# Both tiles' statistics in one group, and one GpSimd product moved to VectorE, in a two-layer diffusion trunk

## The chip, the cores and the metric

One core of one Trainium2 chip runs the whole program in one launch. The metric is device microseconds of one execution. A profiled execution records each engine: TensorE (PE, with its weight loads as PEld), VectorE (DVE), ScalarE (ACT), GpSimd (POOL) and SyncE (SP), which issues DMAs.

## The reference, cut to what matters

Two layers run over 128 prompt tokens and 1024 sample tokens, in float32, with model width 1024. Layer 0 mixes tokens by softmax attention (8 heads) beside a bidirectional gated linear attention (4 heads); layer 1 mixes by a convolution module. A SwiGLU FFN follows each. Every sub-layer begins with a modulation:

```python
def rmsnorm(x, g):
    y = xf * lax.rsqrt(jnp.mean(xf * xf, axis=-1, keepdims=True) + EPS)
    return (y * g.astype(jnp.float32)).astype(x.dtype)
def modulate(x, g, shift, scale):
    return rmsnorm(x, g) * (1 + scale) + shift
```

In the linear attention, per chunk, queries and keys are multiplied by exponentials of summed log gates: `scores = einsum('bhid,bhjd,bhijd->bhij', qc, kc, decay)` with `decay = exp(cum_i - cum_j)`.

## The kernel before, in words

Tokens lie along the free dimension: 1152 tokens are four tiles of 288 columns (after the convolution 280, 280, 296, 296), tiles 0 and 1 being group GA and tiles 2 and 3 group GB. The 1024 features are eight k-blocks of 128 partitions. Every float32 product is three matmuls over operands split in a high and a low part (`mm3`, L161 to L163); a weight block arrives by DMA on SyncE (`wraw`), ScalarE casts it to `wH` (L156), VectorE or GpSimd subtracts to get `wL` (L157).

`modulate` handles a group's two tiles one after the other. Per tile, `x_stats` squares the eight k-blocks on ScalarE (L369, L372) and adds them on VectorE (L373) into a tile `ssum` (two buffers); `bcast_rstd` sums over partitions with small matmuls against ones (L188), takes the reciprocal square root of a few columns (L191, L174 to L179), and spreads it over the partitions with small matmuls against the identity (L196) into a bank of `m` (two PSUM banks in these stages). Then `affine` makes `hH` and `hL` for the eight k-blocks (L381 to L391). The squares and the affine share a scratch tile `tmp` with four buffers. There are six such modulations after layer 0's mix, two tiles each: layer 0 FFN for GA and GB, layer 1 mix for GA and GB, layer 1 FFN for GA and GB.

In `layers`, layer 0's FFN for GA runs in six chunks of hidden blocks; GB's modulation stands after the second. Beside it VectorE sums the modulation parameters from streamed weights (`ada`, L292). Layer 1's convolution has a first product `pw1` with eight blocks f, each followed by a convolution that VectorE does tap by tap (L1275) and that is handed out in portions (`drip`); the FFN of the other group covers it.

In the attention stage (about 490 to 890 us of the span) the main loop is the softmax attention of a head; the linear attention `gla_b` is braided in, one chunk t of 128 tokens after the other (nine chunks). For each of two feature blocks f, ScalarE fills `kq` with exponentials (L904, L911), then `kq` is multiplied in place by the queries and keys: slots 0 to 6 by one product (L913, 896 elements per partition: on VectorE for f = 0, on GpSimd for f = 1), slots 7 to 15 by another (L915, 1152 elements, VectorE). TensorE takes both in the score matmuls (L928), whose results VectorE gathers in `pt` (L931, L933).

A framework sets the order of each engine's instructions at compile time: from the order in the program and from its own estimate of when each operand is ready. An instruction can be moved ahead of earlier ones where the estimate says that it is ready. On the chip each engine then works through its queue in that order, and an instruction that waits holds up those behind it.

Of the kernel before, what the change touches and what calls it, by code (L numbers as in the profile page):

```python
# [14 lines left out]
AF = mybir.ActivationFunctionType  # L15
ALU = mybir.AluOpType
AX = mybir.AxisListType

P = 128
D = 1024  # L20
KD = D // P
# [5 lines left out]
GA, GB = (0, 1), (2, 3)  # L27
# [20 lines left out]
R_PW, R_FF0, R_FF1 = 4, (5, 3), (4, 2)  # L48
# [9 lines left out]
EPS = 1e-6  # L58
# [58 lines left out]
class Trunk:  # L117
# [273 lines left out]
            nc.vector.scalar_tensor_tensor(L[:, k, s:e], t[:, s:e], sh[:, k, g:g + 1], H[:, k, s:e].bitcast(F32),  # L391
                                           op0=ALU.add, op1=ALU.subtract)

    def modulate(self, X, l, which, tts):
        nc = self.nc
        sh, a = self.par[l][3 * which], self.par[l][3 * which + 1]
        hs = {}
        for tt in tts:
            w = X[tt].shape[2]
            bc = self.x_stats(X, tt)  # L400
            H, L = self.h_tiles(tt, w)
            for k in range(KD):
                self.affine(tt, k, X[tt][:, k, :], bc, H, L, sh, a, MODS[k])
            hs[tt] = (H, L)
        return hs
# [467 lines left out]
    def gla_b(self, t):  # L873
        nc, kg, S, tb = self.nc, self.kg, self.S, self.gb
        fs, bs = kg[:, 0:1024], kg[:, 1024:2048]
        NL = len(LEVELS)
        tok = slice(t * P, (t + 1) * P)
        gqk = self.t(tb, [P, 4, P], "gqk", 2)
# [12 lines left out]
        for f in range(2):  # L891
            kq = self.t(tb, [P, 2 * NL + 2, P], "kq", 3)
            for d in range(2):
                src = fs if d == 0 else bs
                for half in range(2):
                    E = self.bank("g")
                    for i, L in enumerate((laH, laL)):
                        nc.tensor.matmul(E, L[:, d * 256 + f * P:d * 256 + (f + 1) * P],
                                         src[:, half * 512:half * 512 + 512], start=(i == 0), stop=(i == 1))
                    for q in range(4):  # L900
                        l = half * 4 + q
                        iv = E[:, q * P:(q + 1) * P]
                        if l == NL:
                            nc.scalar.activation(kq[:, 2 * NL + d, :], iv, AF.Exp)  # L904
                            continue
                        s = LEVELS[l]
                        base = kq[:, l, :] if d == 0 else kq[:, l, s:]
                        st = NL * P + s if d == 0 else NL * P - s
                        ov = bass.AP(base.tensor, base.offset,
                                     [list(base.ap[0]), [st, 2], [2 * s, 64 // s], [1, s]])  # L910
                        nc.scalar.activation(ov, iv.rearrange("p (a b c) -> p a b c", a=2, c=s), AF.Exp)  # L911
                    yield
            (nc.gpsimd if f else nc.vector).tensor_mul(kq[:, 0:NL], kq[:, 0:NL], gqk[:, f, :].unsqueeze(1).to_broadcast([P, NL, P]))  # L913
            yield
            nc.vector.tensor_mul(kq[:, NL:], kq[:, NL:],  # L915
                                 gqk[:, 2 + f, :].unsqueeze(1).to_broadcast([P, NL + 2, P]))
            KQ.append(kq)
            yield
# [19 lines left out]
        for f in range(2):  # L938
            for hp in range(2):
                h = f * 2 + hp  # L940
                nc.tensor.matmul(Ob[hp][:, f, :], PT[hp][:, f, :], gv[:, h * GDV:(h + 1) * GDV],
                                 start=True, stop=(t == 0))
            for d in range(2 if t > 0 else 0):
                for hp, r in enumerate(half):
                    nc.tensor.matmul(Ob[hp][:, f, :], KQ[f][r, 2 * NL + d, :], S(d, t)[r, f, :],
                                     start=False, stop=(d == 1))
        yield
        ss = self.t(tb, [P, GH], "gss", 2)
# [360 lines left out]
    def pw1(self, hs, grp, rate):  # L1309
        nc = self.nc  # L1310
        w1 = self.A["conv_w_pw1"][0].rearrange("(k p) f -> p k f", p=P)
        first = grp is GA
        x, C = self.x_group(T2, grp)
        for f in range(KD):
            bH, bL = self.wtile(w1[:, :, D + f * P:D + (f + 1) * P])
            aH, aL = self.wtile(w1[:, :, f * P:(f + 1) * P])
            u = self.t(self.up, [P, max(UA, UB)], f"u{f}")
            if first:
                nc.gpsimd.memset(u[:, 0:CPAD], 0.0)
                nc.gpsimd.memset(u[:, CPAD + P:2 * CPAD + P], 0.0)  # L1320
            else:
                nc.scalar.copy(u[:, 0:HALO], self.halo[:, f, :])
                nc.gpsimd.memset(u[:, UB - CPAD:UB], 0.0)
            for tt in grp:
                hH, hL = hs[tt]
                w = hH.shape[2]
                ba, bb = self.bank("a")[:, :w], self.bank("a")[:, :w]
                for k in range(KD):
                    self.mm3(bb, bH[:, k], bL[:, k], hH[:, k], hL[:, k], k == 0, k == KD - 1)
                for k in range(KD):  # L1330
                    self.mm3(ba, aH[:, k], aL[:, k], hH[:, k], hL[:, k], k == 0, k == KD - 1)
                sg = self.ev()[:, :w]
                nc.scalar.activation(sg, bb, AF.Sigmoid, bias=self.b_pw1[:, KD + f:KD + f + 1])
                a0 = T1[tt][0]
                parts = [(CPAD, 0, P), (2 * CPAD + P, P, w)] if tt == 0 else \
                    [(a0 + 2 * CPAD if first else a0 - (N2 - CPAD), 0, w)]
                for d, s, e in parts:
                    nc.vector.scalar_tensor_tensor(u[:, d:d + e - s], ba[:, s:e], self.b_pw1[:, f:f + 1],
                                                   sg[:, s:e], op0=ALU.add, op1=ALU.mult)
                self.drip(rate)  # L1340
            if first:
                nc.scalar.copy(self.halo[:, f, :], u[:, UA - HALO:UA])
                self.conv_taps(u, f, [(x[:, f, 0:P], 0), (x[:, f, P:], CPAD + P)])
            else:
                self.conv_taps(u, f, [(x[:, f, :], 0)])
        return C

    def x_load(self, X, grp):
        x, xs = self.x_group(T2, grp)
# [3 lines left out]
    def layers(self, X, hs):  # L1353
        nc, A = self.nc, self.A
        pa = self.pool("act")
        self.wpool = WPOOL[1]
        NB = max(C0A + C0B + C1A + C1B)
        cut = lambda ns: list(zip(np.cumsum((0,) + ns).tolist(), ns))
        chunks = cut(C0A)
        self.adq = nc.sync  # L1360
        self.ada_pin = ADA_PIN
        self.adp = self.pool("ada1", "right")
        self.ada_bufs = AB[2]
        gate = self.ada_seq(0, (5,), 512)
        self.pend.extend([lambda: next(gate, None)] * 20)
        ada = self.ada_seq(1, (1, 0, 2, 4, 3, 5), 512)
        for f0, n in chunks:
            for _ in range(-(-120 // len(chunks))):
                self.pend.append(lambda: next(ada, None))
            self.ffn(X, hs, 0, GA, f0, n, pa, NB, ADA_RATE if f0 else (4, 4))  # L1370
            self.drip(10 ** 6)
            if f0 == chunks[1][0]:
                hs.update(self.modulate(X, 0, 1, GB))
        self.adp.release()
        self.wpool = 0
        gate = self.par[1][2]
        nc.vector.tensor_mul(self.bg, gate, self.b_pw2.unsqueeze(2).to_broadcast([P, KD, 2]))
        w2 = A["conv_w_pw2"][0].rearrange("(k p) f -> p k f", p=P)
        self.up = self.pool("u", "right")
        self.halo = self.t(self.up, [P, KD, HALO], "halo")  # L1380

        hs.update(self.modulate(X, 1, 0, GA))
        self.x_dma(self.xg[0], 0, True)
        chunks = cut(C0B)
        self.ffn(X, hs, 0, GB, *chunks[0], pa, NB)
        C = self.pw1(hs, GA, R_PW)
        for c in chunks[1:-1]:
            self.ffn(X, hs, 0, GB, *c, pa, NB, R_FF0)
        self.drip(10 ** 6)
        self.wpool = WPOOL[3]  # L1390
        us = self.layer_norm(C, GA)
        self.ffn(X, hs, 0, GB, *chunks[-1], pa, NB)
        X2 = {}
        self.x_load(X2, GA)

        hs.update(self.modulate(X, 1, 0, GB))
        self.x_dma(self.xg[1], N1, True)
        self.proj_add(X2, us, w2, GA, gate, self.bg)
        h2 = self.modulate(X2, 1, 1, GA)
        C = self.pw1(hs, GB, R_PW)  # L1400
        chunks = cut(C1A)
        for c in chunks[:-2]:
            self.ffn(X2, h2, 1, GA, *c, pa, NB, R_FF1)
        self.drip(10 ** 6)
        self.wpool = WPOOL[3]
        us = self.layer_norm(C, GB)
        self.x_load(X2, GB)
        self.ffn(X2, h2, 1, GA, *chunks[-2], pa, NB)
        self.proj_add(X2, us, w2, GB, gate, self.bg)
        h2.update(self.modulate(X2, 1, 1, GB))  # L1410
        self.ffn(X2, h2, 1, GA, *chunks[-1], pa, NB)
        self.store_y(X2, GA)
        self.wpool = WPOOL[4]
        self.up.release()
        for c in cut(C1B):
            self.ffn(X2, h2, 1, GB, *c, pa, NB)
        self.store_y(X2, GB)
        pa.release()
# [55 lines left out]
```

## Time and profile before

| | |
|---|---|
| median of three runs | 3096.03 us (3094.78 to 3100.07) |
| the profiled execution | 3098.96 us |
| its span, first to last instruction | 3097.2 us |
| TensorE matmuls busy | 3002.1 us, 97% |
| VectorE busy | 2169.4 us, 70% |
| ScalarE busy | 1232.1 us, 40% |
| GpSimd busy | 405.2 us, 13% |
| mean granted TensorE clock | 0.984 |

Times in rows count from the span's start, in microseconds. A busy share is a mean over stages; what a change is worth is read at the waits of the engine that sets the end. An arrow `<-` behind a wait names what ended it.

### The profile page before, as it was taken

What the parts mean: (1) busy time and instruction counts of PE and PEld (TensorE: products, weight loads), DVE (VectorE), ACT (ScalarE), POOL (GpSimd) and SP (SyncE); (2) the same over time, 40 slices, a digit from 0 to 9 for tenths busy, and PEclk for the clock granted to TensorE, in tenths of its full rate; (3) what the DMA queues carried; (4) which work ended last, traced back from release to release, by engine and by line L of the source; (5) the groups of instructions that cost most, each with busy time, mean ns of one, the idle gap of its engine ahead of it and who ended that gap; (6) DMA issues with size and microseconds to landing.
All of it is one profiled execution on the core that took longest, in us unless ns stands there. A gap on an engine that the chain in (4) does not pass through costs nothing.

```text
span 3097.2 us, 53660 instructions
## 1 busy us (share of the span) xinstructions
PE 3002.1 (97%) x21044; PEld 2813.7 (91%) x21044; DVE 2169.4 (70%) x4110; ACT 1232.1 (40%) x2652; POOL 405.2 (13%) x371
## 2 busy tenths in 40 slices
PE   7999999999989999999999999999999999999999
PEld 4999866666769999999999999999999999999998
DVE  6668478788769999634679996667888875433343
ACT  5323377566664333223422223562222255222222
POOL 1012121112120111111111110111111010000000
PEclk9999999999999999999999999999999999999999
DMA  7545522111164555423232222522322231322222
GB/s 266 169 120 149 156 88 70 55 46 52 26 188 151 168 157 155 127 82 103 80 86 83 78 82 76 149 69 83 89 86 86 83 113 51 110 82 83 81 86 78
DMA packets 449631, 320.46 MB, mean 103 GB/s; under 512 B 29646, under 2 KB 413907, under 8 KB 449378
## 3 DMA queue, kind: packets, MB, share of 16 engines
q1 hardware_dynamic: 411726, 271.06, 29.3%
q0 software_dynamic: 8944, 30.68, 3.1%
q10 hardware_dynamic: 28708, 15.29, 1.7%
q8 instruction: 166, 2.72, 0.4%
q14 instruction: 87, 0.71, 0.1%
HBM read 278.30 MB, written 38.67 MB: 102 GB/s over the span
## 4 chain that ended last, share of the span: by engine, by line
PE 75%; DVE 13%; ACT 5%; DMA 3%; issue 3%; POOL 0%; SPq 0%; ACTq 0%; DVEq 0%; POOLq 0%
PE ps_a L161 16%; PE ps_a L163 16%; PE ps_a L162 16%; PE ps_d L162 3%; PE ps_d L163 3%; PE ps_d L161 3%; DVE y L1275 2%; PE ps_g L928 2%; PE ps_a L538 2%; PE ps_a L540 2%; PE ps_a L539 2%; DVE ada L292 1%; DVE wL L157 1%; DVE x L409 1%; PE ps_c L1236 1%
## 5 line engine op out<-in xcount | busy, mean ns | idle before, releaser
L163 PE MATMUL ps_a<-hH,wL 128*128 128x288 f32 (+2 forms) x3328 | 985.3, 296 | 6.7 <-DVE wL L157 6.7
L161 PE MATMUL ps_a<-hH,wH 128*128 128x288 f32 (+2 forms) x3328 | 983.9, 296 | 1.8 <-ACT wH L156 1.8
L162 PE MATMUL ps_a<-hL,wH 128*128 128x288 f32 (+2 forms) x3328 | 985.2, 296 | 0.0
L156 ACT CAST wH<-wraw 128x1024 fp32r<-128x1024 f32 (+3 forms) x432 | 362.4, 843 | 768.4 <-PE ps_a L162 480.7
L163 PEld LDWEIGHTS ps_a<-hH,wL 128*128 128x128 f32 x3328 | 627.7, 189 | 8.0 <-DVE wL L157 7.8
L161 PEld LDWEIGHTS ps_a<-hH,wH 128*128 128x128 f32 x3328 | 629.0, 189 | 2.6 <-ACT wH L156 2.3
L162 PEld LDWEIGHTS ps_a<-hL,wH 128*128 128x128 f32 x3328 | 627.5, 189 | 0.2
L157 DVE TENSOR_TENSOR wL<-wraw,wH 128x1024 fp32r<-128x1024 f32 (+3 forms) x349 | 336.0, 965 | 130.2 <-ACT wH L156 129.3
L1275 DVE SCALAR_TENSOR_TENSOR y<-u,cvw,y 128x575 f32<-128x575 f32 (+1 forms) x464 | 420.1, 905 | 8.4
L157 POOL TENSOR_TENSOR wL<-wraw,wH 128x1024 fp32r<-128x1024 f32 (+2 forms) x83 | 172.7, 2081 | 975.3 <-ACT wH L156 975.1
L161 PE MATMUL ps_a<-aH,wH 128*128 128x288 f32 (+2 forms) x880 | 259.8, 296 | 0.2 <-ACT wH L156 0.2
L163 PE MATMUL ps_a<-aH,wL 128*128 128x288 f32 (+2 forms) x880 | 259.0, 295 | 0.0
L162 PE MATMUL ps_a<-aL,wH 128*128 128x288 f32 (+2 forms) x880 | 258.9, 294 | 0.0
L448 DVE TENSOR_TENSOR ev<-ev,ps_a 128x288 f32<-128x288 f32 (+2 forms) x176 | 79.3, 450 | 226.9 <-PE ps_a L163 225.6
L292 DVE SCALAR_TENSOR_TENSOR ada<-ada,scc,ada 128x512 f32<-128x512 f32 (+1 forms) x364 | 219.7, 647 | 20.0 <-DMA ada<-in_w_ada 19.8
L156 ACT CAST aH<-ev 128x288 fp32r<-128x288 f32 (+2 forms) x176 | 75.9, 431 | 330.7 <-DVE ev L448 329.1
L161 PEld LDWEIGHTS ps_a<-aH,wH 128*128 128x128 f32 x880 | 165.9, 189 | 0.5 <-ACT wH L156 0.5
L162 PEld LDWEIGHTS ps_a<-aL,wH 128*128 128x128 f32 x880 | 166.1, 189 | 0.0
L163 PEld LDWEIGHTS ps_a<-aH,wL 128*128 128x128 f32 x880 | 165.5, 188 | 0.5 <-DVE wL L157 0.5
L161 PE MATMUL ps_d<-aH,wH 128*128 128x288 f32 (+2 forms) x528 | 158.3, 300 | 6.3 <-ACT wH L156 3.5
L161 PE MATMUL ps_d<-hH,wH 128*128 128x288 f32 (+2 forms) x512 | 153.2, 299 | 8.6 <-DVE dr L1248 6.6
L409 DVE SCALAR_TENSOR_TENSOR x<-ps_a,par,x 128x288 f32<-128x288 f32 (+5 forms) x300 | 128.5, 450 | 45.8 <-PE ps_a L163 45.1
(338 smaller groups left out, 5770.7 us busy)
## 6 DMA issues: line engine op xcount, KB each, us to landing
wraw<-in_ffn_w_gate SPq DMA_DIRECT2D x88, 512.0 KB
wraw<-in_ffn_w_up SPq DMA_DIRECT2D x88, 512.0 KB
wraw<-in_ffn_w_down SPq DMA_DIRECT2D x144, 256.0 KB
ada<-in_w_ada SPq DMA_DIRECT2D x112, 256.0 KB
wraw<-in_conv_w_pw SPq DMA_DIRECT2D x48, 512.0 KB
in<-in_w_ada SPq DMA_DIRECT2D x8, 1024.0 KB
ada<-in_w_ada SPq DMA_DIRECT2D x64, 128.0 KB
wraw<-in_w_out SPq DMA_DIRECT2D x16, 512.0 KB
```

What stands on the lines that cost most here:

```text
L156: self.nc.scalar.copy(H, src)
L157: (eng or self.nc.vector).tensor_sub(L, src, H.bitcast(F32))
L161: mm(out, WH, hH, start=start, stop=False)
L162: mm(out, WH, hL, start=False, stop=False)
L163: mm(out, WL, hH, start=False, stop=stop)
L292: ins = self.nc.vector.scalar_tensor_tensor(acc[v], w, s, acc[v], op0=ALU.mult, op1=ALU.add)
L409: self.nc.vector.scalar_tensor_tensor(X[tt][:, o, s:e], src[:, s:e], gate[:, o, g:g + 1], X[tt][:, o, s:e], op0=ALU.mult, op1=ALU.add)
L448: nc.vector.tensor_mul(pr, sl, bu)
L538: mm(b[:, :wd], hh, wh, start=(k == 0), stop=False)
L539: mm(b[:, :wd], hh, wl, start=False, stop=False)
L540: mm(b[:, :wd], hl, wh, start=False, stop=(k == KD - 1))
L1275: pin(nc.vector.scalar_tensor_tensor(d, u[:, i + o:i + o + w], c, y[:, o:o + w], op0=ALU.mult, op1=ALU.add))
```

## The change

Two independent edits. `modulate` now takes the squares and sums of both tiles first (`sums`), then treats them in one group (`pair_bcast`): one set of small matmuls, one square root and one chain of short VectorE instructions over the columns of both tiles, and two broadcast banks. In two of the six places the halves are pulled apart: for GB in layer 0 the sums stand after the second FFN chunk and the rest after the third; for GA in layer 1's FFN the sums stand before the second `pw1` and the rest after its first block, for which `pw1` has become a generator. In `gla_b`, the product of L913 is on VectorE for both f.

```diff
+    def pair_bcast(self, sums, w):
...
+        st = self.bank()
+        for i, s in enumerate(sums):
+            for j in range(n):
+                o = 2 * (i * n + j)
+                nc.tensor.matmul(st[:c, o:o + 2], s[:, j * c:(j + 1) * c], self.ones[:, 0:2], start=True, stop=True)
+        m = n * len(sums)
+        tmp = self.tmp()
+        v, r, q = (tmp[:c, i:i + m] for i in (0, 8, 16))
...
+        nc.scalar.activation(q, v, AF.Sqrt)
+        nc.vector.reciprocal(r, q)
...
+        for i in range(len(sums)):
+            bc = self.bank()
+            for j in range(n):
+                nc.tensor.matmul(bc[:, j * c:(j + 1) * c], r[:c, i * n + j:i * n + j + 1].to_broadcast([c, P]),
+                                 self.ident[:c, :c], start=True, stop=True)
...
+    def sums(self, X, tts):
...
+            nc.scalar.activation(ssum, x[:, 0, :], AF.Square)
+            for k in range(1, KD):
+                sq = self.tmp()[:, :w]
+                nc.scalar.activation(sq, x[:, k, :], AF.Square)
+                nc.vector.tensor_add(ssum, ssum, sq)
...
-    def modulate(self, X, l, which, tts):
+    def modulate(self, X, l, which, tts, ss=None):
...
-        for tt in tts:
+        ss = ss or self.sums(X, tts)
+        for tt, bc in zip(tts, self.pair_bcast(ss, X[tts[0]].shape[2])):
             w = X[tt].shape[2]
-            bc = self.x_stats(X, tt)
...
-            (nc.gpsimd if f else nc.vector).tensor_mul(kq[:, 0:NL], kq[:, 0:NL], gqk[:, f, :].unsqueeze(1).to_broadcast([P, NL, P]))
+            nc.vector.tensor_mul(kq[:, 0:NL], kq[:, 0:NL], gqk[:, f, :].unsqueeze(1).to_broadcast([P, NL, P]))
...
             if f0 == chunks[1][0]:
-                hs.update(self.modulate(X, 0, 1, GB))
+                ss = self.sums(X, GB)
+            if f0 == chunks[2][0]:
+                hs.update(self.modulate(X, 0, 1, GB, ss))
...
-        h2 = self.modulate(X2, 1, 1, GA)
-        C = self.pw1(hs, GB, R_PW)
+        ss = self.sums(X2, GA)
+        pw = self.pw1(hs, GB, R_PW)
+        C = next(pw)
+        next(pw)
+        h2 = self.modulate(X2, 1, 1, GA, ss)
+        for _ in pw:
+            pass
```

## Rows read from the trace of the kernel before

**Rows 1.** The page, part 1: busy us, share, instructions of each engine.
```profile
PE 3002.1 (97%) x21044; PEld 2813.7 (91%) x21044; DVE 2169.4 (70%) x4110; ACT 1232.1 (40%) x2652; POOL 405.2 (13%) x371
```

**Rows 2.** TensorE's waits: us in total, times, longest us.
```profile
PE ps_m L188 <- DVE ssum L373: 8.7, 7, 3.1
...
PE ps_g L928 <- DVE kq L915: 4.5, 4, 1.6
```

**Rows 3.** Stretches: length; busy us (instructions) of PE, PEld, DVE, ACT, POOL; clock; DMA.
```profile
490.00:890.00 400.00, 378.56 (x1935) 271.21 (x1934) 311.74 (x641) 254.21 (x735) 84.51 (x69) 0.95 0.19 58
...
1142.00:1219.00 77.00, 71.91 (x523) 71.26 (x522) 68.84 (x132) 36.75 (x70) 15.58 (x12) 0.96 0.42 131
1219.00:1296.00 77.00, 77.00 (x588) 77.00 (x588) 61.96 (x103) 23.14 (x38) 10.85 (x6) 1.00 0.50 151
```

**Rows 4.** Lines 913 and 915: ns min/median/max, first and last start.
```profile
L913 POOL TENSOR_TENSOR kq<-kq,gqk x9: 2087/2405/2617, 504.9 to 863.5; 128x896 f32<-128x896 f32 x9
...
L915 DVE TENSOR_TENSOR kq<-kq,gqk x18: 1342/1486/3267, 499.8 to 863.8; 128x1152 f32<-128x1152 f32 x18
```

**Rows 5.** Timeline around the products: start, us, engine, line, operation [idle before].
```profile
498.82 1.09 DVE L913 TENSOR_TENSOR kq<-kq,gqk 128x896 f32<-128x896 f32 x1
499.83 1.35 DVE L915 TENSOR_TENSOR kq<-kq,gqk 128x1152 f32<-128x1152 f32 x1
...
504.91 2.62 POOL L913 TENSOR_TENSOR kq<-kq,gqk 128x896 f32<-128x896 f32 x1 [2.42 <-ACT kq L911]
505.51 3.23 DVE L915 TENSOR_TENSOR kq<-kq,gqk 128x1152 f32<-128x1152 f32 x1
508.89 0.34 PE L928 MATMUL ps_g<-kq 64*128 64x128 f32 x1 [0.96 <-DVE kq L915]
...
633.66 0.37 PE L928 MATMUL ps_g<-kq 64*128 64x128 f32 x1 [0.69 <-DVE pt L931]
...
717.17 3.18 DVE L915 TENSOR_TENSOR kq<-kq,gqk 128x1152 f32<-128x1152 f32 x1
720.50 0.34 PE L928 MATMUL ps_g<-kq 64*128 64x128 f32 x1 [1.53 <-DVE kq L915]
...
770.44 3.23 DVE L915 TENSOR_TENSOR kq<-kq,gqk 128x1152 f32<-128x1152 f32 x1
773.82 0.34 PE L928 MATMUL ps_g<-kq 64*128 64x128 f32 x1 [1.62 <-DVE kq L915]
...
815.57 2.56 POOL L913 TENSOR_TENSOR kq<-kq,gqk 128x896 f32<-128x896 f32 x1
818.49 1.35 DVE L915 TENSOR_TENSOR kq<-kq,gqk 128x1152 f32<-128x1152 f32 x1
```

**Rows 6.** Four stretches at the lower clock, columns as in Rows 3.
```profile
721.20:731.50 10.30, 10.30 (x36) 6.76 (x34) 6.24 (x12) 3.91 (x8) 3.35 (x3) 0.50 0.30 79
...
775.90:789.50 13.60, 13.60 (x59) 9.66 (x59) 5.14 (x13) 2.05 (x4) 0.06 (x1) 0.50 0.00 0
...
1168.40:1171.80 3.40, 3.40 (x16) 3.40 (x15) 3.40 (x9) 2.11 (x3) 0.00 (x0) 0.50 0.28 82
...
2079.70:2083.20 3.50, 3.50 (x18) 3.50 (x18) 0.57 (x2) 0.62 (x2) 0.00 (x0) 0.51 0.44 125
```

**Rows 7.** Timeline of squares and TensorE in three modulations, columns as in Rows 5.
```profile
1161.32 1.88 ACT L372 ACTIVATE tmp<-x 128x288 f32<-128x288 f32 x4 [0.58 <-POOL hL L157]
...
1166.40 0.39 PE L188 MATMUL ps_m<-ones,ssum 128*96 128x2 f32 x3 [3.12 <-DVE ssum L373]
...
2074.80 2.29 ACT L372 ACTIVATE tmp<-x 128x280 f32<-128x280 f32 x6
...
2079.21 0.45 PE L188 MATMUL ps_m<-ones,ssum 128*70 128x2 f32 x5 [2.33 <-DVE ssum L373]
...
1482.48 0.40 PE L161 MATMUL ps_a<-hH,wH 128*128 128x288 f32 x1 [1.38 <-ACT wH L156]
```

**Rows 8.** Groups by line, 960 to 2630 us: count, busy us, mean ns, idle before.
```profile
L174 ACT ACT_TABLE_LOAD x13 | 16.7, 1283 | 0.2
```

More of the change, by code (lines that the diff above doesn't have):

```diff
@@ L392, in affine @@
                                            op0=ALU.add, op1=ALU.subtract)
-    def modulate(self, X, l, which, tts):
+    def pair_bcast(self, sums, w):
+        nc = self.nc
+        n = next(i for i in range(-(-w // P), w) if w % i == 0)
+        c = w // n
+        st = self.bank()
[6 more added lines that the diff above has]
+        v, r, q = (tmp[:c, i:i + m] for i in (0, 8, 16))
+        nc.vector.tensor_scalar(v, st[:c, 0:2 * m].rearrange("p (a b) -> p a b", b=2)[:, :, 0], 1.0 / D, EPS,
+                                op0=ALU.mult, op1=ALU.add)
+        nc.scalar.activation(q, v, AF.Sqrt)
+        nc.vector.reciprocal(r, q)
+        nc.vector.tensor_mul(q, r, r)
+        nc.vector.tensor_mul(q, q, v)
+        nc.vector.tensor_scalar(q, q, -0.5, 1.5, op0=ALU.mult, op1=ALU.add)
+        nc.vector.tensor_mul(r, r, q)
+        out = []
+        for i in range(len(sums)):
[3 more added lines that the diff above has]
+                                 self.ident[:c, :c], start=True, stop=True)
+            out.append(bc[:, :w])
+        return out
+    def sums(self, X, tts):
+        nc = self.nc
+        out = []
+        for tt in tts:
+            x = X[tt]
+            w = x.shape[2]
+            ssum = self.t(self.tp, [P, self.sw], "ssum", 2)[:, :w]
+            nc.scalar.activation(ssum, x[:, 0, :], AF.Square)
[3 more added lines that the diff above has]
+                nc.vector.tensor_add(ssum, ssum, sq)
+            out.append(ssum)
+        return out
+    def modulate(self, X, l, which, tts, ss=None):
         nc = self.nc
@@ L1313, in pw1 @@
         x, C = self.x_group(T2, grp)
+        yield C
         for f in range(KD):
@@ L1345, in pw1 @@
                 self.conv_taps(u, f, [(x[:, f, :], 0)])
-        return C
+            yield
     def x_load(self, X, grp):
@@ L1385, in layers @@
         self.ffn(X, hs, 0, GB, *chunks[0], pa, NB)
-        C = self.pw1(hs, GA, R_PW)
+        C = [c for c in self.pw1(hs, GA, R_PW) if c][0]
         for c in chunks[1:-1]:
```

## The prediction

> **What bounds the kernel now.** I read the page's busy shares first: TensorE is busy 97% of the span, VectorE 70%, ScalarE 40%, GpSimd 13% [rows 1]. So the time can only fall where TensorE stands still or runs at the lower of its two clocks. The second view is TensorE's waits. Two of its rows belong to what the change touches: the small matmuls of L188 wait 8.7 us in seven places for the sum of squares, and L928 waits 4.5 us in four places for the second product on `kq` [rows 2]. The third view is the table by stretches: in the attention stage, 490 to 890 us, TensorE idles 400.00 - 378.56 = 21.4 us and its mean clock is 0.95, while VectorE is busy 312 us, 78% [rows 3]. The fourth view is the timeline around each of these waits, and there the causes show.
>
> **Part 1, the product of L913 for f = 1 goes from GpSimd to VectorE.** On GpSimd one takes 2405 ns (median of nine) [rows 4]. VectorE begins L915 for the same f shortly after it. Where the two overlap, L915 is slow: 3.23 us at 505.51, 3.18 at 717.17, 3.23 at 770.44, and each time it ends 1.2 us behind the GpSimd product's end where that is shown (504.91 + 2.62 = 507.53, against 508.74). Where it started only after GpSimd was done (815.57 + 2.56 = 818.13, against 818.49), it took 1.35 us, as it does for f = 0 with nothing beside it (499.83) [rows 5]. So GpSimd's product holds VectorE up by about 1.9 us, and moving it costs VectorE less than it frees: for f = 0 both products on VectorE take 498.82 to 501.18, 2.36 us in all, and after the change f = 1 should too. Counted from the old start of L915, `kq` is ready 3.23 - 2.36 = 0.87 us earlier at the first chunk.
>
> TensorE waited right there in five chunks: 0.96, 1.53 and 1.62 us, a fourth that is the rest of the 4.5 us (0.36) [rows 2, 5], and 0.69 at 633.66, where the releaser named is L931, queued on VectorE behind a slow L915 [rows 5]. Each gets back the smaller of its wait and its gain: 0.87 + 0.82 + 0.87 (gain), 0.36 and 0.69 (whole wait) = 3.6 us. Bounds: none, if other VectorE work moves into the freed time, and below nothing if L915 stays slow (a rival). At 818.49 `kq` will be ready about 1.0 us later; TensorE had no wait there. What is late next in two chunks is still L915, by 0.7 us.
>
> [...]
>
> [...]
>
> **Part 2, the statistics of both tiles together.** In the kernel before, the second tile's squares need `tmp` buffers that the first tile's affine holds. At 1161.32 four squares in a row start when GpSimd's `hL` step gives one back, and TensorE, which reached the second L188 in its queue, waits 3.12 us; at 2074.80 six squares in a row, and 2.33 us [rows 7]. With `sums` ahead of the affine in the program the squares of both tiles come first in that rotation, and follow each k-block as it is finished. The waits should go. Of the 8.7 us I leave 0.2 us per modulation, 1.2 us, for the one group that still has to wait for the last block: gain 7.5 us (bounds 0 and 8.7). Both waits named are followed by a stretch at 0.50, 3.4 and 3.5 us [rows 6]; half of it comes back, 3.4 us. Here matmuls stand back to back on both sides, so I count it whole.
>
> What is added and removed otherwise: the small matmuls are the same in number, since each tile has the same columns. One square root and one chain of short VectorE steps per modulation go, and with the root one load of an activation table at 1283 ns [rows 8] and the load back. ScalarE is off the path except in one place: at 1482.48 TensorE waits 1.38 us for a weight cast (L156) that sits behind six squares of the second tile [rows 7]. Those squares now come earlier; I take half, 0.7 us.
>
> Pulling apart costs nothing as long as matmuls cover it. For GB in layer 0 the affine of two tiles moves from the stretch 1142 to 1219 into 1219 to 1296. There VectorE is busy 62 of 77 us [rows 3], so it becomes as full as the first stretch was (69 of 77), and the first gets room: a shift, counted as nothing. GB's tiles are needed only after the sixth chunk. GA's tiles for layer 1's FFN are needed after the seven remaining blocks of `pw1`. No DMA is issued by the moved steps; on GpSimd the four `hL` subtractions per tile move along, an engine 13% busy. Both banks of `m` are now held through both affines, so an L317 sum of modulation parameters behind them can wait for a bank; nothing of before shows that, and I bound it from 0 to the longest L188 wait, 3.1 us [rows 2], and take 0, because the next such sum comes a chunk later.
>
> **Sum.** 3.6 + 6.0 + 7.5 + 3.4 + 0.7 = 21.2 us off the profiled execution's 3098.96 us gives 3077.8. That execution lies 2.9 us above the median of the runs shown (3096.03). From the middle of the two, 3097.5, the sum gives 3076, my forecast.
>
> **The rivals.** [...] (2) The wait moves instead of going: the compile-time order puts the one L188 group as early as its estimate of the sums allows, VectorE is late again, and TensorE waits as long once as it did twice. [...] For it: the estimate was wrong in seven places before; against it: at the two dear places other work now stands between sums and group. (3) Slower: VectorE binds attention. It is busy 78% there [rows 3]. If L915 for f = 1 is slow for another reason than GpSimd, the product of 1.09 us [rows 5] goes in front of it and `kq` comes 1.0 us later in nine chunks: 9 us more waiting, and, if four more chunks then drop to the lower clock for 5 to 7 us of loss each as two did, 24 us. With part 2's 11.6 lost nowhere: 3097.5 + 9 + 24 - 11.6 = 3119. It decides from the point where L915 for f = 1 still takes over 3 us. Against it stands the one L915 that ran alone.
>
> [...]
>
> **How the numbers follow.** A run of this kernel can tell about 0.2%, 6.2 us, from no change: faster is below 3089.8, slower above 3102.2. Forecast, 3076: 0.52. Rival 1, 3082: 0.18. Rival 2: 0.19, half at 3087 and half at 3093. Rival 3, 3119: 0.11. Faster: 0.52 + 0.18 less a few hundredths for their upper ends, plus part of the 0.09 at 3087: 0.73. Same: 0.16. Slower: 0.11. The range ends low where every term is whole (3.6 + 12.0 + 8.7 + 3.4 + 1.4 = 29.1, 3068) less some 10 us for what a new order of instructions can give; it ends high at 3097, above rival 2 with (1). Rival 3 is left out.
>
> **What would show it.** Right: every L915 near 1.35 us; L928's waits for `kq` under 1 us each, and no long stretch at 0.50 right behind them; L188 waiting in fewer places, none over 1 us; six square roots fewer. Wrong: L915 over 2 us for f = 1; an L188 or L196 wait of 2 us or more in a modulation; a longer wait of L928 on `pt`; new waits for `wL` around 1219 to 1300 us, where VectorE becomes full.

## The result, and the profile after

The changed kernel takes 3075.82 us (median of four runs, 3072.86 to 3077.35) against 3095.41 us (four runs): a ratio of 0.9933 [0.9921, 0.9946], 19.6 us less. The forecast was 3076. The total came out; two parts of the sum did not, and they cancelled. In the profiled executions the span fell by 23.1 us: 17.7 us in the attention stage, about nothing behind it, and the rest ahead of it, where the code is the same.

Line numbers of the changed kernel: L913 and L915 are now L957 and L959, L928 is L972, and L933, which makes `pt`, is L977; the modulations' small matmuls are L402 and L418, their squares' sums L434.

The page's busy shares, columns as in [rows 1]:

```profile
PE 2984.6 (97%) x21044; PEld 2804.4 (91%) x21044; DVE 2160.9 (70%) x4083; ACT 1225.7 (40%) x2640; POOL 385.5 (13%) x362
```

TensorE is busy 17.5 us less with the same instructions, so the clock, not only the waiting, changed: 0.984 in the mean of the span before, 0.988 now. ScalarE has 12 instructions fewer: six square roots and six table loads. The two lines of the change, columns as in [rows 4]:

```profile
L957 DVE TENSOR_TENSOR kq<-kq,gqk x18: 1071/1084/1614, 494.4 to 843.1; 128x896 f32<-128x896 f32 x18
L959 DVE TENSOR_TENSOR kq<-kq,gqk x18: 1342/1350/1354, 495.4 to 844.1; 128x1152 f32<-128x1152 f32 x18
```

All eighteen L959 now take 1.35 us. In total, busy us and mean ns, first before and then after:

```profile
L915 DVE TENSOR_TENSOR kq<-kq,gqk 128x1152 f32<-128x1152 f32 x18 | 37.7, 2094 | 0.0
L959 DVE TENSOR_TENSOR kq<-kq,gqk 128x1152 f32<-128x1152 f32 x18 | 24.3, 1350 | 0.0
```

The attention stage, from the first matmul of the linear attention into `ps_g` to the last of softmax attention into `ps_c`; columns as in [rows 3]; first the kernel before, cut at the same matmuls:

```profile
490.60:894.90 404.30, 381.86 (x1946) 273.02 (x1944) 313.35 (x645) 257.95 (x743) 85.79 (x70) 0.95 0.19 57
```

Then the changed kernel, with the two stretches at the lower clock in this stage and the three at the new waits below:

```profile
485.50:872.10 386.60, 368.00 (x1946) 263.94 (x1944) 305.01 (x651) 258.69 (x741) 61.08 (x61) 0.99 0.20 60
...
584.30:591.10 6.80, 6.80 (x32) 4.16 (x29) 3.98 (x10) 1.37 (x3) 1.60 (x2) 0.50 0.28 86
488.70:492.10 3.40, 3.40 (x10) 2.47 (x9) 2.67 (x7) 2.94 (x13) 0.00 (x0) 0.50 0.24 77
...
2072.50:2079.30 6.80, 4.56 (x19) 4.56 (x20) 4.85 (x3) 0.00 (x0) 2.19 (x1) 0.50 0.48 133
...
1461.50:1464.90 3.40, 3.40 (x16) 3.40 (x15) 3.40 (x6) 2.85 (x7) 2.55 (x2) 0.50 0.13 39
...
1150.90:1154.30 3.40, 3.40 (x17) 3.40 (x16) 3.32 (x6) 2.07 (x4) 0.00 (x0) 0.50 0.79 235
```

Length less busy PE is idle time: 22.4 us before, 18.6 after. So 3.8 of the 17.7 us are waiting. The other 13.9 us are busy time at the same matmuls (381.86 to 368.00): the clock. The stretches at 0.50 add up to 41.0 and 10.2 us. Half of them, 20.5 and 5.1, is the loss by the prediction's way of counting, an estimate; its difference, 15.4, is somewhat more than the busy time shows. VectorE has nine products more of the first kind (9.8 us at L913 before, 20.0 at L957 after) and is yet busy 8.3 us less. The second product alone fell by 13.4 us. The remaining 5.1 us lie in other VectorE instructions, which are not followed here.

TensorE's waits, columns as in [rows 2]:

```profile
PE ps_a L163 <- DVE wL L157: 10.6, 6, 2.2
...
PE ps_a L163 <- POOL wL L157: 5.0, 1, 5.0
...
PE ps_a L161 <- ACT wH L156: 2.6, 1, 2.6
...
PE ps_g L972 <- DVE pt L977: 0.7, 2, 0.4
...
PE ps_m L402 <- DVE ssum L434: 0.4, 2, 0.2
```

The 8.7 us in seven places at L188 have become 0.4 us in two at L402, and L928's 4.5 us for `kq` are gone. But weight waits have come: 5.0 us for a GpSimd `wL`, 2.6 us for a `wH`, and two more for a VectorE `wL` (6.7 us in four places before, 10.6 in six now). Behind the attention stage no gain shows, first in the kernel before and then in the changed one (from 20 us after that last matmul to the end, columns as in [rows 3]):

```profile
915.20:3097.20 2182.00, 2147.24 (x16136) 2133.89 (x16134) 1515.43 (x2575) 742.38 (x1330) 241.96 (x187) 0.99 0.33 99
```

```profile
892.50:3074.10 2181.60, 2146.28 (x16139) 2134.82 (x16138) 1515.03 (x2541) 734.75 (x1318) 246.66 (x187) 0.99 0.33 100
```

(The kernel with the products alone, below, which has the old modulations, takes 2188.40 us there. So two traces can be 6 us apart in this part with the same source.)

The timeline around the new waits, columns as in [rows 5]; four pieces, one after the other, two from layer 0's FFN, one from layer 1's mixing and one from layer 1's FFN:

```profile
1143.16 5.53 DVE L292 SCALAR_TENSOR_TENSOR ada<-ada,scc,ada 128x512 f32<-128x512 f32 x5
...
1148.62 1.21 DVE L157 TENSOR_TENSOR wL<-wraw,wH 128x1024 fp32r<-128x1024 f32 x1
...
1149.88 0.40 PE L163 MATMUL ps_a<-hH,wL 128*128 128x288 f32 x1 [2.21 <-DVE wL L157]
...
1242.89 3.77 DVE L292 SCALAR_TENSOR_TENSOR ada<-ada,scc,ada 128x512 f32<-128x512 f32 x4
...
1247.85 0.40 PE L163 MATMUL ps_a<-hH,wL 128*128 128x288 f32 x1 [1.69 <-DVE wL L157]
...
1450.86 0.72 ACT L390 ACTIVATE hH<-tmp,par 128x128 fp32r<-128x128 f32 x2 [2.40 <-DVE tmp L388]
...
1460.10 1.03 ACT L156 CAST wH<-wraw 128x1024 fp32r<-128x1024 f32 x1
...
1461.18 0.40 PE L161 MATMUL ps_a<-hH,wH 128*128 128x288 f32 x1 [2.63 <-ACT wH L156]
...
2067.57 0.80 POOL L157 TENSOR_TENSOR hL<-tmp,hH 128x280 fp32r<-128x280 f32 x1 [0.90 <-ACT hH L156]
2069.76 2.10 POOL L157 TENSOR_TENSOR hL<-tmp,hH 128x280 fp32r<-128x280 f32 x1 [1.38 <-ACT hH L156]
2071.82 2.87 POOL L157 TENSOR_TENSOR wL<-wraw,wH 128x1024 fp32r<-128x1024 f32 x1
...
2074.74 0.61 PE L163 MATMUL ps_a<-hH,wL 128*128 128x288 f32 x1 [4.95 <-POOL wL L157]
```

At 1149.88 and 1247.85 a weight's `wL` comes behind VectorE's sums of modulation parameters (L292, 5.53 and 3.77 us in one piece). The modulation itself does not stand there: in this trace the squares of layer 0's second group run from 971.5 to 998.1 us, and its affine from 1210.9 to 1226.8. At 2074.74 another case: the wait of 2.33 us for the second tile's squares [rows 7] is gone, and 4.95 us stand some 18 us further on in the program. The affine steps of both tiles now run in one piece, GpSimd works through their `hL`, and the weight's `wL` is queued on it behind the last: TensorE had used the `wH` of that weight at 2069.36, and GpSimd stood idle for 1.38 us before 2069.76 until an `hH` came. At 1461.18 the `wH` cast (1460.10) stands on ScalarE behind the affine of the first tile's eight blocks, which begins at 1450.86, after the squares of both tiles (1421.2 to 1442.4). The kernel before waited 1.38 us at the same place. Three of the four waits have a stretch at 0.50 around or behind them, 6.8, 3.4 and 3.4 us in the rows above, in place of the 3.4 and 3.5 of [rows 6]; the one at 1247.85 has none.

### The profile page after: what moved, and what is told of

Same layout as the page of the kernel before. It is cut to its first block, busy times and chain, and to the rows that moved or that the text cites. A ratio compares the mean times of both kernels' runs of the same rounds, so it can differ in the third digit from the quotient of the medians.

```text
span 3074.1 us, 53580 instructions
## 1 busy us (share of the span) xinstructions
PE 2984.6 (97%) x21044; PEld 2804.4 (91%) x21044; DVE 2160.9 (70%) x4083; ACT 1225.7 (40%) x2640; POOL 385.5 (13%) x362
## 3 DMA queue, kind: packets, MB, share of 16 engines
q1 hardware_dynamic: 411726, 271.06, 29.5%
## 4 chain that ended last, share of the span: by engine, by line
PE 77%; DVE 11%; ACT 5%; DMA 3%; issue 3%; POOL 1%; ACTq 0%; SPq 0%; DVEq 0%; POOLq 0%
PE ps_a L161 16%; PE ps_a L163 16%; PE ps_a L162 16%; PE ps_d L161 3%; PE ps_d L162 3%; PE ps_d L163 3%; DVE y L1319 2%; PE ps_g L972 2%; DVE ada L292 2%; PE ps_a L582 2%; PE ps_a L583 2%; PE ps_a L584 2%; DVE wL L157 1%; DMA ada<-in_w_ada 1%; PE ps_p L1242 1%
## 5 line engine op out<-in xcount | busy, mean ns | idle before, releaser
L163 PE MATMUL ps_a<-hH,wL 128*128 128x288 f32 (+2 forms) x3328 | 986.2, 297 | 15.6 <-DVE wL L157 10.6
L161 PE MATMUL ps_a<-hH,wH 128*128 128x288 f32 (+2 forms) x3328 | 985.3, 296 | 2.7 <-ACT wH L156 2.6
L163 PEld LDWEIGHTS ps_a<-hH,wL 128*128 128x128 f32 x3328 | 629.2, 189 | 17.6 <-DVE wL L157 12.3
L161 PEld LDWEIGHTS ps_a<-hH,wH 128*128 128x128 f32 x3328 | 630.4, 189 | 3.4 <-ACT wH L156 3.2
L161 PE MATMUL ps_a<-aH,wH 128*128 128x288 f32 (+2 forms) x880 | 259.4, 295 | 0.0
L163 PE MATMUL ps_a<-aH,wL 128*128 128x288 f32 (+2 forms) x880 | 259.0, 295 | 0.0
L292 DVE SCALAR_TENSOR_TENSOR ada<-ada,scc,ada 128x512 f32<-128x512 f32 (+1 forms) x364 | 226.0, 667 | 23.3 <-DMA ada<-in_w_ada 23.2
L161 PEld LDWEIGHTS ps_a<-aH,wH 128*128 128x128 f32 x880 | 165.7, 188 | 0.0
L163 PEld LDWEIGHTS ps_a<-aH,wL 128*128 128x128 f32 x880 | 165.4, 188 | 0.1
L161 PE MATMUL ps_d<-aH,wH 128*128 128x288 f32 (+2 forms) x528 | 157.3, 298 | 6.0 <-ACT wH L156 3.5
L161 PE MATMUL ps_d<-hH,wH 128*128 128x288 f32 (+2 forms) x512 | 154.5, 302 | 7.4 <-DVE dr L1292 6.0
```

The lines of the kernel that those rows point to most:

```text
L161: mm(out, WH, hH, start=start, stop=False)
L163: mm(out, WL, hH, start=False, stop=stop)
L292: ins = self.nc.vector.scalar_tensor_tensor(acc[v], w, s, acc[v], op0=ALU.mult, op1=ALU.add)
```

## The experiments

**Which half of the change carries the gain.** One kernel has only the products (before, with both on VectorE), one only the statistics (the changed kernel, with f = 1 back on GpSimd).

```diff
 # e1_product: the kernel before
-            (nc.gpsimd if f else nc.vector).tensor_mul(kq[:, 0:NL], ...)
+            nc.vector.tensor_mul(kq[:, 0:NL], ...)
 # e2_stats: the changed kernel
-            nc.vector.tensor_mul(kq[:, 0:NL], ...)
+            (nc.gpsimd if f else nc.vector).tensor_mul(kq[:, 0:NL], ...)
```

> The kernel before with the product of L913 on VectorE for both f; the modulations as before. Theory A (the prediction's sum): 9.6 us off, ratio 0.9969. Theory B (read from the two profiles: the attention stage became 17.7 us shorter, the modulations together 0.3 us): 17 to 20 us off, ratio 0.9940. Theory C (most of the attention stage's gain is the clock's chance of one execution): 3 to 6 us off. All expect every L915 near 1.35 us; B expects under 15 us at the lower clock in attention, A some 25.

> The changed kernel with the product for f = 1 back on GpSimd; statistics in pairs and pulled apart as in the change. Theory A (the prediction's sum): 11.6 us off the kernel before, ratio 0.9963. Theory B: the waits at the statistics' small matmuls go, but waits for weights behind two tiles' affine take their place (4.95, 2.63 and 2.21 us in the changed kernel's profile), so 0 to 4 us off, ratio 0.999 to 1.000. L915 for f = 1 should take about 3.2 us again where GpSimd runs beside it.

Products alone: 0.9943 [0.9926, 0.9959], 3081.38 us against 3097.79, which is theory B. Statistics alone: 0.9989 [0.9978, 1.0001], by the ratio 3.4 us less with an interval from 6.8 less to 0.3 more. The two lines, the waits of interest and the attention stage, of products alone:

```profile
L915 DVE TENSOR_TENSOR kq<-kq,gqk x18: 1344/1350/1352, 499.9 to 848.7; 128x1152 f32<-128x1152 f32 x18
```

```profile
PE ps_m L188 <- DVE ssum L373: 8.8, 7, 3.1
```

```profile
490.80:876.60 385.80, 367.00 (x1945) 263.01 (x1944) 305.41 (x651) 258.25 (x741) 60.57 (x61) 0.99 0.20 60
```

and of statistics alone:

```profile
L957 POOL TENSOR_TENSOR kq<-kq,gqk x9: 2084/2399/2622, 501.3 to 859.8; 128x896 f32<-128x896 f32 x9
L959 DVE TENSOR_TENSOR kq<-kq,gqk x18: 1344/1488/3257, 496.4 to 860.2; 128x1152 f32<-128x1152 f32 x18
```

```profile
PE ps_a L163 <- POOL wL L157: 5.0, 1, 5.0
...
PE ps_g L972 <- DVE kq L959: 4.8, 5, 1.6
```

```profile
486.50:891.20 404.70, 382.34 (x1945) 273.20 (x1944) 313.27 (x644) 258.39 (x743) 85.90 (x70) 0.95 0.19 57
```

They separate cleanly. Products alone has the attention stage of the changed kernel (385.8 us, clock 0.99) with all of L188's waits kept; statistics alone has that of the kernel before (404.7 us, 0.95, L972's waits for `kq` back), and already the 5.0 us wait for GpSimd's `wL`.

**Is it GpSimd that slows VectorE's product, or something in f = 1?** The engines swapped (f = 0 on GpSimd), and both products on GpSimd.

```diff
 # e3_swap: the changed kernel
-            nc.vector.tensor_mul(kq[:, 0:NL], ...)
+            (nc.vector if f else nc.gpsimd).tensor_mul(kq[:, 0:NL], ...)
 # e4_both_gpsimd: the changed kernel
-            nc.vector.tensor_mul(kq[:, 0:NL], ...)
+            nc.gpsimd.tensor_mul(kq[:, 0:NL], ...)
```

> The changed kernel, with the product of L913 on GpSimd for f = 0 and on VectorE for f = 1. Theory B (GpSimd's product holds VectorE's up wherever the two overlap): L915 takes 2.5 to 3.3 us for f = 0 and 1.35 for f = 1, and the time goes back towards the kernel before's attention, unless f = 0 has more slack: 5 to 18 us over the changed kernel. Rival (it was something about f = 1, such as what it is queued with): L915 for f = 0 stays at 1.35 and the time is that of the changed kernel within 3 us.

> The changed kernel with the product of L913 on GpSimd for both f. Theory B: eighteen GpSimd products, nearly every L915 at 2.7 to 3.3 us, VectorE busy some 15 us more than with nine, and the time 10 to 35 us over the changed kernel. Rival (VectorE has room in attention, and only the order of f = 1 mattered): no more than 3 us between this and the swapped kernel.

Swapped: 0.9962 [0.9949, 0.9974], some 9 us over the changed kernel, as expected. Both on GpSimd: 1.0072 [1.0054, 1.009], 3120.06 us, so slower than the kernel before and 44 us over the changed one, more than the 10 to 35 expected. Swapped, first the two lines, then L959's busy total and mean ns, a wait, and the stage:

```profile
L957 POOL TENSOR_TENSOR kq<-kq,gqk x9: 2103/2122/3242, 501.5 to 849.7; 128x896 f32<-128x896 f32 x9
L957 DVE TENSOR_TENSOR kq<-kq,gqk x9: 1073/1081/2178, 510.6 to 858.3; 128x896 f32<-128x896 f32 x9
L959 DVE TENSOR_TENSOR kq<-kq,gqk x18: 1344/1352/3230, 501.8 to 859.3; 128x1152 f32<-128x1152 f32 x18
```

```profile
L959 DVE TENSOR_TENSOR kq<-kq,gqk 128x1152 f32<-128x1152 f32 x18 | 36.3, 2018 | 7.7 <-ACT kq L948 7.7
```

```profile
PE ps_c L1280 <- DVE pL L157: 8.2, 8, 2.3
```

```profile
493.20:887.20 394.00, 366.84 (x1946) 263.27 (x1945) 311.88 (x643) 259.44 (x741) 86.20 (x70) 0.99 0.20 59
```

Both on GpSimd, the two lines and the stage:

```profile
L957 POOL TENSOR_TENSOR kq<-kq,gqk x18: 2078/2114/3993, 494.6 to 879.8; 128x896 f32<-128x896 f32 x18
L959 DVE TENSOR_TENSOR kq<-kq,gqk x18: 1341/3018/3287, 495.2 to 882.4; 128x1152 f32<-128x1152 f32 x18
```

```profile
485.80:921.60 435.80, 396.27 (x1946) 282.73 (x1945) 317.55 (x636) 260.29 (x745) 108.36 (x79) 0.91 0.18 54
```

The slow product follows GpSimd, not f. Swapped, all nine f = 1 products take 1.35 us and seven of the nine f = 0 products 2.80 to 3.23; with both on GpSimd the median of all eighteen is 3.02. VectorE then issues nine or eighteen products fewer and is busier for it: 317.55 us against 305.01.

The stage by kernel, from the window rows (idle is length less busy PE) and from the stretches at 0.50:

| kernel | length | TensorE busy | TensorE idle | at 0.50 |
|---|---|---|---|---|
| before | 404.3 | 381.9 | 22.4 | 41.0 |
| changed | 386.6 | 368.0 | 18.6 | 10.2 |
| products alone | 385.8 | 367.0 | 18.8 | 6.8 |
| statistics alone | 404.7 | 382.3 | 22.4 | 44.4 |
| swapped | 394.0 | 366.8 | 27.2 | 6.8 |
| both on GpSimd | 435.8 | 396.3 | 39.5 | 78.5 |

How much clock came back differs from execution to execution. Nine kept traces have both products on VectorE: the changed kernel twice, products alone, and the six of the variants below. In them the stage takes 385.8 to 389.4 us, with 18.4 to 18.8 us idle, 367.0 to 370.8 busy and 6.8 to 17.1 at 0.50. The changed kernel's second trace is near the upper end:

```profile
485.30:874.50 389.20, 370.64 (x1946) 266.47 (x1944) 305.04 (x651) 258.95 (x741) 60.98 (x61) 0.98 0.20 59
```

So against the kernel before 11 to 15 us of busy time came back beside some 4 us of waiting.

Swapped, TensorE idles more than before, 11.2 us of it at L1280, the value product of softmax attention, and the clock still stays up. So the idle sum does not set the clock loss. What about the waits, or the matmuls around them, decides it stays open.

**Does pulling the statistics apart from the affine matter?** One kernel with layer 1's FFN modulation in one piece again, one with layer 0's too; the changed kernel ran beside them.

```diff
 # e6_apart_gb, and e5_no_apart
-        ss = self.sums(X2, GA)
+        h2 = self.modulate(X2, 1, 1, GA)
         pw = self.pw1(hs, GB, R_PW)
         C = next(pw)
-        next(pw)
-        h2 = self.modulate(X2, 1, 1, GA, ss)
 # e5_no_apart alone
             if f0 == chunks[1][0]:
-                ss = self.sums(X, GB)
-            if f0 == chunks[2][0]:
-                hs.update(self.modulate(X, 0, 1, GB, ss))
+                hs.update(self.modulate(X, 0, 1, GB))
```

> The changed kernel itself, again, beside the variants of this call: ratio 0.9933 as before, within 0.0015, and at layer 1's FFN modulation for GA again a wait of TensorE of about 5 us for a low weight part made on GpSimd.

> The changed kernel, but layer 1's FFN modulation for GA stands whole ahead of the second pw1, in pairs, not pulled apart. Theory B (pulled apart, the affine of both tiles meets the taps of the convolution, and the weight part that GpSimd makes lies behind eight hL steps): the 4.95 us wait and the stretch of 6.8 us at the lower clock behind it go, 3 to 8 us faster than the changed kernel. Rival A (ahead of pw1, the one statistics group has no cover, TensorE waits there as before): L402 waits 2 us or more there and the time is that of the changed kernel within 2 us.

> The changed kernel with pairs, but neither modulation pulled apart (layer 0's for GB also whole, after the second chunk). Theory B: what pulling apart bought in layer 0 was about nothing (the waits moved from L188 to weights behind the parameter sums), so within 3 us of the variant that leaves only layer 0's apart. Theory A: the L402 group waits 2 to 3 us at the second chunk's end, with 1.7 us of lower clock behind it: 3 to 5 us slower than that variant.

Changed kernel again 0.9947 [0.9935, 0.996], one in one piece 0.9949 [0.9936, 0.9961], both 0.9959 [0.9946, 0.9971]: not told apart. The 3 to 8 us that I expected of the one in one piece did not come. TensorE's waits from 2050 to 2180 us of the kernel with only layer 1's FFN in one piece say why:

```profile
PE ps_a L163 <- DVE wL L157: 3.6, 1, 3.6
...
PE ps_a L161 <- DVE u L1383: 2.0, 1, 2.0
```

The 4.95 us wait is exchanged for 3.6 and 2.0. Whether the sixteen affine blocks come in one piece before `pw1` or behind its first block, a weight's preparation ends up behind them. The kernel with both in one piece has no wait at the places of 1149.88 and 1247.85, but one of 1.95 us for a `wL` at 1192.1.

**So deal the affine out.** `modulate` becomes a generator that yields after each k-block. In `e7_spread`, three blocks of layer 1's FFN modulation follow each `pw1` block. `e9_spread2_apart` also hands out those of layer 1's mixing, one or two k-blocks at a time, within the next FFN chunk of layer 0. `e8_spread2` is the same with layer 0's second group no longer pulled apart.

```diff
 # e7_spread, e9_spread2_apart and e8_spread2
                 self.affine(tt, k, X[tt][:, k, :], bc, H, L, sh, a, MODS[k])
+                yield
...
+        ms = self.mod_steps(X2, 1, 1, GA, ss, h2)
         C = next(pw)
         next(pw)
-        h2 = self.modulate(X2, 1, 1, GA, ss)
         for _ in pw:
+            for _ in range(3):
+                next(ms, None)
 # e9_spread2_apart and e8_spread2
-        hs.update(self.modulate(X, 1, 0, GA))
+        h1 = {}
+        ms = self.mod_steps(X, 1, 0, GA, None, h1)
+        self.pend.extend([lambda: next(ms, None)] * 17)
+        self.drip(1)
...
-        self.ffn(X, hs, 0, GB, *chunks[0], pa, NB)
+        self.ffn(X, hs, 0, GB, *chunks[0], pa, NB, (2, 1), True)
+        self.drip(10 ** 6)
+        hs.update(h1)
```

> The changed kernel, with the affine of layer 1's FFN modulation for GA dealt out, three k-blocks after each block of pw1 from the second on, the statistics where the change has them. Theory B: no weight lies behind more than three affine steps, the 4.95 us wait and the lower clock behind it go, 5 to 8 us faster than the changed kernel. Rival (VectorE is simply full there, taps and affine together): waits for low weight parts of 1 to 3 us in several blocks of pw1 in its place, and no gain.

> The kernel that deals out layer 1's FFN affine for GA, again, as the comparison for the two beside it: ratio 0.993 to 0.995, 0 to 5 us less than the changed kernel.

> The kernel that deals out layer 1's FFN affine for GA, with layer 1's mixing affine for GA dealt out in the same way: two k-blocks at a time inside the FFN chunk that follows it, so that its weight casts do not lie behind sixteen affine steps. Theory B: TensorE's 2.63 us wait for the cast there (and a stretch of 3.4 us at the lower clock behind it) goes, 2 to 4 us less than with one place dealt out, about 7 us less than the changed kernel (ratio to the kernel before about 0.992). Rival: the wait moves to the activations of that chunk (aH, aL), and nothing is gained.

> The same with both places dealt out, and layer 0's modulation for GB not pulled apart. If pulling apart bought nothing there, the same as with it, within 2 us; if it bought the wait at the group's first matmuls, 3 us slower.

`e7_spread`: 0.9943 [0.9927, 0.9959] and, in a second run beside the next two, 0.9929 [0.9913, 0.9944]: not told from the changed kernel, where I had expected 5 to 8 us less. `e9_spread2_apart`: 0.9915 [0.9899, 0.9931]. `e8_spread2`: 0.9909 [0.9892, 0.9925], 3068.31 us against 3096.60. These two are not told apart, so pulling layer 0's group apart buys nothing that the runs can tell. Of the waits from 2050 to 2180 us, `e7_spread` keeps

```profile
PE ps_m L418 <- DVE tmp L413: 1.1, 1, 1.1
```

and no weight wait. The 444 matmul triples (L161 to L163) around this modulation take 184.6 us against 188.7 in the changed kernel and 186.0 in the one before; timed as a whole that is too little to tell. With mixing dealt out too, the program behind attention is shorter, here in `e8_spread2`:

```profile
893.40:3064.40 2171.00, 2141.50 (x16136) 2128.22 (x16136) 1512.59 (x2539) 734.69 (x1318) 249.54 (x187) 1.00 0.34 100
```

It is 10.6 us less than in the changed kernel: 35.3 - 29.5 = 5.8 us of waiting, and 4.8 us of busy time at the same matmuls, which is clock. `e9_spread2_apart` has 2171.7 us there, the other eleven kept traces 2177 to 2188. The waits of both show neither the 4.95 nor the 2.63 us. `e8_spread2` is the version that beats both kernels. Against the changed one the ratios' quotient is 0.9909 / 0.9933 = 0.998, 0.24% with about 0.21% of uncertainty; with the second run of the changed kernel (0.9947) it is 0.38%. Both quotients go by way of the kernel before, and not by runs beside each other.

## Why the prediction was right, and where it was not

**Right: VectorE's product was held up by GpSimd.** The 1.9 us that a GpSimd product cost VectorE were predicted from one lone and several overlapped L915. In the whole trace of the kernel before, eight of the nine for f = 1 were held up, by 0.65 to 1.92 us, 1.64 in the mean, and the swap moved the effect with the engine. Waits removed: 3.6 us predicted, 3.8 in the trace (3.6 with products alone). That agreement is of the net: all 4.5 us of L928's waits for `kq` went, where the sum left 0.7 us in each of two places, and among others 1.5 us came for `mneg` at L1007. Rival 3, a VectorE that binds attention, fell with the first row of L959. (Rival 2, the sum without part 2's 11.6 us, is at 3088, and at 3094 without the 6.0 us of clock as well, not at 3087 and 3093.)

In the trace of the kernel before, each L915 that took more than 1.4 us, nine of them, ends 1.21 or 1.22 us behind the end of a GpSimd instruction that had begun before it. The others, with none running when they began, took 1.34 or 1.35 us. One of the slow ones is for f = 0, 1.62 us at 577.64, and the GpSimd instruction there is not L913 but a subtraction of 0.52 us (577.52). GpSimd pays as well: in the changed kernel, its `hL` at 2069.76 takes 2.10 us, with a `wL` of VectorE from 2070.02 to 2071.23, against 0.80 for the one before it.

**Right in kind, wrong in size: the clock of attention.** No run shows the term of 6.0 us in the sum. It was an estimate: half of the 12.0 us that the two stretches of 10.3 and 13.6 us [rows 6] cost if each costs half its length. What the traces show in its place is 13.9 us less busy time in the changed kernel's, and 11 to 15 in the nine with this attention. The step that failed is the count of what may come back: the estimate took only the stretches behind the two longest waits, and left out a stretch of 13.7 us from 584.7 and one of 3.4 from 656.4 that shrank or went as well. The first stands right behind a wait of 0.70 us, also at L928 (columns as in [rows 5] and [rows 6]):

```profile
582.87 0.49 PE L928 MATMUL ps_g<-kq 64*128 64x128 f32 x2 [0.70 <-DVE pt L931]
...
584.70:598.40 13.70, 13.70 (x53) 9.38 (x54) 9.43 (x18) 5.63 (x12) 3.11 (x4) 0.50 0.22 67
```

I had taken it from two places that waits this short cost no clock: behind the 0.96 us at 508.89 and the 0.69 at 633.66 the clock is 1.00 (508 to 515 and 633.3 to 640). At 582.87 it did not hold. Nor does the wait alone decide: the stretch from 656.4 begins at a wait of 1.90 us at L1226, and the changed kernel keeps that wait, 1.89 us, without a stretch. Rival 1, at 3082 the sum without the 6.0 us, is refuted: attention keeps 18.6 of 22.4 us of idling in short waits, yet the time at 0.50 fell from 41.0 us to between 6.8 and 17.1. The swapped kernel, with 27.2 us idle and 6.8 at 0.50, goes against it too.

**Wrong: part 2.** 7.5 us of L188's waits, 3.4 of clock and 0.7 of the `wH` cast were counted: 11.6. Measured alone, the statistics gave 3.4 us (6.8 less to 0.3 more), and the changed kernel's trace shows 0.4 in this part of the program, where two traces can differ by 6. The waits named did go; rival 2 happened, though not by the way I gave it. I had TensorE wait once for late statistics. Instead the statistics are on time, and weights are late: in layer 1 behind the affine, which for both tiles now runs in one piece, and in layer 0 behind the parameter sums. The step "pulling apart costs nothing as long as matmuls cover it" asked only when the tiles are needed, not what is queued on ScalarE, VectorE and GpSimd behind the moved and merged work. The `wH` wait, cut by half in the sum, went from 1.38 to 2.63 us. Of the signs I listed, "new waits for `wL` around 1219 to 1300" came, 1.69 us at 1247.85, though behind the parameter sums and 20 us after the affine that I had in mind. Dealing out supports the cause in layer 1: `e8_spread2` has neither of the two long waits, and its median is 7.5 us under the changed kernel's. What moved the waits in layer 0 was not tested by itself.

**Chance.** The kernel's first 485 us, which nothing changed, were 5.1 us shorter in the profiled execution, with 6.8 us at the lower clock from 451.1 where before had 13.7 from 455.0. Over the thirteen kept traces this beginning lasts 484 to 493 us, so a single trace against a single trace can be off by more than this; the timed medians carry the verdict. The sum, 21.2 us, and the 19.6 measured agree by luck: part 1 was 9.6 in the sum and measured 16 to 18, and part 2 was 11.6 and measured 3.4 with an interval that takes in none.

## What to carry to other kernels

Two products of one chain on VectorE can beat one on each of VectorE and GpSimd (here medians of 1.08 and 1.35 us, against 2.00 to 3.27 us in eight of nine chunks beside GpSimd's 2.09 to 2.62): compare the slow instruction's duration alone and overlapped before handing work to GpSimd. When a burst of preparation is moved or merged, ask of each engine's queue which weight stands behind it, and deal it out block by block instead. Around a wait, add up all stretches at the lower clock in the stage, not only those behind the longest waits: here 3.8 us less waiting came with 13.9 us of clock.

## What the runs showed of the hardware

VectorE's product L915 took longer where it began beside a running product or subtraction of GpSimd. In the kernel before, all nine that did so end 1.21 or 1.22 us after that GpSimd instruction, whether they had been held up by 0.27 us or by 1.92; the nine others took 1.34 or 1.35 us. No run shows why.

In the traces before and after, the clock granted to TensorE is 1.00 or 0.50 in every stretch. It changed by more than the waits, and not in step with them. In the attention stage 3.8 us less idle time went along with 13.9 us less busy time at the same matmuls, and with both products on GpSimd 17.1 us more (39.5 against 22.4) with 14.4 us more. But 4.8 us more idle, in the swapped kernel, went along with 15.0 us less. I had expected the loss to follow the waits in each case; it did not.
